# State-space tables as outer products of shared power tables, with masks and signs on ScalarE

## The chip, the cores and the metric

The kernel runs on one core of one Trainium2 chip. The core has five engines that run their own instruction queues side by side: TensorE (PE; its weight loads are PEld), VectorE (DVE), ScalarE (ACT), GpSimd (POOL) and SyncE (SP), which issues the DMAs. The metric is the device time of one execution in microseconds, lower is better. All numbers are fp32.

## The reference, cut to what matters

The model is a trunk of two residual layers over 1024 positions and 1024 features: attention beside a short convolution, a gated feed-forward, a state-space mixer, a second gated feed-forward. Only the parameters of the state-space mixer are touched here:

```
dt = exp(log_step); mag = exp(lr * dt)
ar, ai = mag * cos(li * dt), mag * sin(li * dt)
zr, zi = (nr * lr + ni * li) / den, (ni * lr - nr * li) / den
bbar_r = zr * b_re - zi * b_im ; bbar_i = zr * b_im + zi * b_re
state[s] = a * state[s-1] + bbar @ u[s]        (complex, 64 groups of 16 channels, 64 states each)
y[s] = c_re @ state_r[s] - c_im @ state_i[s] + d_skip * u[s]
```

The kernel runs this scan in chunks of 8 steps. For that it needs tables: `bbar * a^k` and `c * a^k` for k = 0 to 8, and for every group a rotation table with 128 powers of the phase of `a^8`, one for each chunk.

## The kernel before, in words

Activations stay transposed in eight tiles `xT[f]` of 128 features by 1024 positions. Every large product is made in three passes of split operands. A *unit* (`mm_unit`, L175) gives 128 channels by 1024 positions in two PSUM banks `pu` out of 48 matmuls of 128x512. A `down` step (L190) adds two hidden rows into all eight `xT[f]`, 12 matmuls and two PSUM banks `pd` for each f, and VectorE adds the banks to `xT` (L193).

The first feed-forward runs 11 groups of four units and, from the second group on, one `down`: gate, value, gate, value, down. VectorE takes each unit out of PSUM (L759, which frees its two banks), filters it (L757, L762, L764) and multiplies the value with the gate (L808). GpSimd makes low parts of weights (`wl`, L154) and of the gated product (`gl`, L810). PSUM has eight banks, so PE can run ahead of VectorE by eight banks and no more.

Beside this, the state-space tables are computed as a background: the generator `stages()` is advanced by one stage at eight places of each group (`background`): ahead of each of the four units, and after every second f of the down. `base()` prepares the powers of `a`, `z` and the phases `w` in rows of 128x32 (a few stages). Then come 16 *units of the tables*, `unit(q)`, of three stages each, and 16 *turns*, `turns(q)`, of one stage each. A scheduler puts the rows of all of this into one order for each engine, and every engine works off its order strictly in sequence.

In `unit(q)` the tile `z[j]` (j: real, imaginary) holds inputs (w = 0) and outputs (w = 1) for two pairs of groups and nine powers. It is filled by doubling: `cmul` is a complex product of six VectorE rows (L1042 to L1047), and it is called with `a`, `a^2`, `a^4` on 64, 128 and 256 columns, then with `a^8` for the last power. PE turns part of it (`pet`, L1085); VectorE changes a sign (L1092) and forms masked copies `bd` (L1096); PE multiplies both into `pk` (L1102); ScalarE copies `pk`, and stores leave. `turns(q)` fills 128 columns from eight by four more `cmul`.

Of the kernel before, what the change touches and what calls it, by code (L numbers as in the profile page):

```python
# [44 lines left out]
# first columns of the gains and filters  # L45
# [5 lines left out]
def hybrid_trunk_kernel(ctx: ExitStack, tc: tile.TileContext, xt, gains, mix_w_in, w_uq, w_ukv, q_gain, k_gain,  # L51
# [129 lines left out]
    def down(gts, ws, after=None, skip=0):  # L181
        """Adds the products of the rows of ws; the first row is left out for the first skip blocks of features."""
# [14 lines left out]
    class Boundary:  # L197
        """Splits x * gain for the products and gathers the row statistics."""
# [22 lines left out]
        def stats(self):  # L221
            """Row statistics; the function returned broadcasts them to all partitions."""
# [10 lines left out]
    def first_units(ws, xs, bd, rbpool):  # L233
        """Three units beside the row statistics: the first two as the inputs appear."""
# [72 lines left out]
    pps.close()  # L307
    with phase("pc") as pC, tc.tile_pool(name="psa", bufs=1, space=PSUM, reuse_waits="tile") as pa:
# [8 lines left out]
        # compressed projections, natural layout  # L317
# [35 lines left out]
        # up-projection weights of queries, keys and values  # L353
# [14 lines left out]
        def c_products(kind, p):  # L368
            """Compressed queries, or keys and values, of two blocks of rows."""
# [61 lines left out]
        class Step:  # L431
            """Queries, keys and values of two heads and half of the rows."""
# [139 lines left out]
        class Item:  # L572
            """One head and one block of queries."""
# [64 lines left out]
        def row_down(k, f):  # L638
            """One block of features of the output projection's rows k."""
# [107 lines left out]
    def ffn(layer, bd, rbpool, open_pool, gtile, down_last, background=lambda: None, first=None):  # L747
# [30 lines left out]
        def unit():  # L778
            """The next unit's products; the weights of the one after it are made ready before they are used."""
# [65 lines left out]
    class Params:  # L845
# [10 lines left out]
        def held(self):  # L856
            """A value of the preparation alone."""
# [89 lines left out]
        def base(self):  # L947
# [30 lines left out]
            for k in (2, 4, 8):  # L978
                self.a[k] = self.square(self.a[k // 2], (self.t(f"a{k}r"), self.t(f"a{k}i")), False)
            # zero-order hold factor  # L980
# [15 lines left out]
            # chunk decay and chunk rotation  # L996
# [13 lines left out]
            # zero part of the chunk kernel, skip weights  # L1010
# [16 lines left out]
        def cmul(self, dst, src, a, sl, n, eng, rep=1):  # L1027
            """dst = src * a, with a per pair of groups, n columns each."""
# [9 lines left out]
            for j in range(4):  # L1038
                c = self.pool.tile([P, 256], F32, tag=f"cm{j}", name=f"cm{j}")[:, 0:rep * q * n]
# [7 lines left out]
            eng.tensor_tensor(out=dst[1], in0=t[2], in1=t[3], op=ALU.add)  # L1047

# [9 lines left out]
        def unit(self, q):  # L1058
            sl = slice(2 * q, 2 * q + 2)
            bt, ct = self.loaded  # L1060
            # (inputs | outputs), pair, power, channel
            z = [self.pool.tile([P, 2, 2, 9, GC], F32, tag=f"z{j}", name=f"z{j}") for j in range(2)]
            ps = psum("pct")
            nc.tensor.transpose(ps[:, 0:64], ct.rearrange("p j s -> p (j s)"), ident[0:64, 0:64])
            pv = ps[:, 0:64].rearrange("p (t g c) -> p t g c", t=2, g=2)
            for j in range(2):
                for g in range(2):
                    nc.scalar.activation(z[j][64 * g:64 * g + 64, 1, :, 0, :], pv[64 * j:64 * j + 64, :, g, :], AF.Copy)
            self.cmul([z_[:, 0, :, 0, :] for z_ in z], bt, self.z, sl, GC, V)
# [4 lines left out]
            for k in (1, 2, 4):  # L1074
                n = GC * k
                self.cmul([z_[:, :, :, n:2 * n] for z_ in zf], [z_[:, :, :, 0:n] for z_ in zf],
                          self.a[k], sl, n, V, rep=2)
            self.cmul([z_[:, 1, :, 8, :] for z_ in z], [z_[:, 1, :, 0, :] for z_ in z], self.a[8], sl, GC, V)
            yield
            # inputs to chunk states, turned  # L1080
# [10 lines left out]
            # kernel of the chunk  # L1091
            V.tensor_scalar(out=z[1][:, 1], in0=z[1][:, 1], scalar1=-1.0, scalar2=None, op0=ALU.mult)  # L1092
            bd = [self.pool.tile([P, 2, 2, GC], F32, tag=f"bd{j}", name=f"bd{j}") for j in range(2)]
            for j in range(2):
                for g in range(2):
                    V.tensor_scalar(out=bd[j][:, :, g, :], in0=z[j][:, 0, :, 0, :], scalar1=self.hv[:, g:g + 1],  # L1096
                                    scalar2=None, op0=ALU.mult)
# [11 lines left out]
            def store():  # L1109
# [3 lines left out]
                # chunk states to outputs  # L1113
# [10 lines left out]
        def turns(self, q):  # L1124
            """Rotation table of two pairs of groups."""
            sl = slice(2 * q, 2 * q + 2)
            wt = [self.pool.tile([P, 2, NCH], F32, tag=f"wt{j}", bufs=2, name=f"wt{j}") for j in range(2)]
            for j in range(2):
                V.tensor_copy(out=wt[j][:, :, 0:8], in_=self.w8[j][:, sl, :])
            for k in (8, 16, 32, 64):  # L1130
                self.cmul([w_[:, :, k:2 * k] for w_ in wt], [w_[:, :, 0:k] for w_ in wt], self.w[k], sl, k, V)
# [10 lines left out]
        def run(self):  # L1142
            """The stages; what a stage stores leaves at the start of the next one."""
# [6 lines left out]
        def stages(self):  # L1150
            yield from self.base()
            self.loaded = self.load(0)
            yield
# [5 lines left out]
            V.memset(self.w8[0][:, :, 0:1], 1.0)  # L1159
            V.memset(self.w8[1][:, :, 0:1], 0.0)  # L1160
            for k in (1, 2, 4):
                self.cmul([x_[:, :, k:2 * k] for x_ in self.w8], [x_[:, :, 0:k] for x_ in self.w8],
                          self.w[k], slice(0, NP), k, V)
# [46 lines left out]
    ud = dp.tile([KT, P, L, NCH], F32, name="ud")  # L1210
    gd = dp.tile([KT, P, L, NCH], F32, name="gd")
    with ExitStack() as p5s:
# [4 lines left out]
        def enter(m, ps):  # L1217
            """Inputs of 128 channels, to be turned by way of memory."""
# [10 lines left out]
        def turn_inputs(m):  # L1229
            """The inputs of 128 channels with the steps of a chunk on the partitions."""  # L1230
# [23 lines left out]
        def states(m):  # L1254
            """States at the chunks' starts: the chunks' inputs, turned, scanned and turned back."""
# [104 lines left out]
        def gated(j, k0, k1):  # L1360
            """Part of one of the gated unit's first products."""
# [77 lines left out]
def layout(inputs):  # L1439
    """The inputs as the kernel takes them: features on the rows of x, all gains and filters as columns."""  # L1440
# [43 lines left out]
```

## Time and profile before

| what | value |
|---|---|
| time, median of 3 runs (lowest, highest) | 2395.21 us (2392.81, 2395.78) |
| span of the profiled execution | 2393.0 us |
| PE busy | 2308.6 us, 96% |
| VectorE busy | 1585.3 us, 66% |
| ScalarE, GpSimd busy | 776.4 us, 790.9 us |
| mean granted PE clock | 0.984 of full speed |

The span runs from the first instruction to the last of one profiled execution; the time of a run is measured from outside. No time of its own is recorded for the profiled execution; the median of the runs lies 2.2 us above its span. Busy shares are means over stages whose limits differ.

### The profile page before, as it was taken

What the parts mean: (1) busy time and instruction counts of PE and PEld (TensorE: products, weight loads), DVE (VectorE), ACT (ScalarE), POOL (GpSimd) and SP (SyncE); (2) the same over time, 40 slices, a digit from 0 to 9 for tenths busy, and PEclk for the clock granted to TensorE, in tenths of its full rate; (3) what the DMA queues carried; (4) which work ended last, traced back from release to release, by engine and by line L of the source; (5) the groups of instructions that cost most, each with busy time, mean ns of one, the idle gap of its engine ahead of it and who ended that gap; (6) DMA issues with size and microseconds to landing.
All of it is one profiled execution on the core that took longest, in us unless ns stands there. A gap on an engine that the chain in (4) does not pass through costs nothing.

```text
span 2393.0 us, 30439 instructions
## 1 busy us (share of the span) xinstructions
PE 2308.6 (96%) x11492; PEld 1922.9 (80%) x11492; DVE 1585.3 (66%) x3202; ACT 776.4 (32%) x1290; POOL 790.9 (33%) x539
## 2 busy tenths in 40 slices
PE   8999899999999999999999978999999999999999
PEld 6889888888778777787878867788888888888887
DVE  6344677786978878888988487333565665555655
ACT  4112565664223222222223255322322222222221
POOL 3321444444223222222215344333232323322320
PEclk9999999999999999999999998999999999999999
DMA  4111000012112222223332387411111101111111
GB/s 152 44 46 46 1 10 10 10 54 71 37 54 77 66 70 68 51 73 85 93 93 75 103 228 232 116 53 44 53 49 49 51 29 53 53 54 44 53 44 71
DMA packets 215282, 159.57 MB, mean 67 GB/s; under 512 B 24352, under 2 KB 199776, under 8 KB 215136
## 3 DMA queue, kind: packets, MB, share of 16 engines
q1 hardware_dynamic: 215136, 157.63, 22.9%
q8 instruction: 90, 1.47, 0.3%
q14 instruction: 56, 0.46, 0.1%
HBM read 131.44 MB, written 30.34 MB: 68 GB/s over the span
## 4 chain that ended last, share of the span: by engine, by line
PE 56%; DVE 8%; DMA 2%; issue 2%; POOL 1%; ACT 1%; SPq 0%; DVEq 0%; POOLq 0%; ACTq 0%
PE pu L175 38%; PE pd L190 16%; DVE c L764 1%; DMA cs<-csd 1%; DVE c L762 1%; DVE cm L1042 1%; DVE xT L193 1%; DVE cm L1045 1%; DVE cm L1044 1%; DVE c L808 1%; DVE u L759 0%; DMA raw<-in_ffn_w_up_dram 0%; DVE cm L1043 0%; POOL ss L1285 0%; PE pk L1102 0%
## 5 line engine op out<-in xcount | busy, mean ns | idle before, releaser
L154 POOL TENSOR_TENSOR wl<-raw,wh 128x1024 fp32r<-128x1024 f32 (+1 forms) x181 | 448.8, 2481 | 919.5 <-ACT wh L153 376.3
L175 PE MATMUL pu<-f_h,wh 128*128 128x512 f32 x1408 | 437.6, 392 | 0.0
L175 PE MATMUL pu<-f_h,wl 128*128 128x512 f32 x1408 | 435.4, 390 | 0.0
L175 PE MATMUL pu<-f_l,wh 128*128 128x512 f32 x1408 | 434.5, 390 | 0.0
L153 ACT ACTIVATE wh<-raw 128x1024 fp32r<-128x1024 f32 (+1 forms) x183 | 192.1, 1054 | 653.5 <-PE pu L175 406.7
L193 DVE TENSOR_TENSOR xT<-pd,xT 128x512 f32<-128x512 f32 x400 | 254.4, 682 | 106.2 <-PE pd L190 105.8
L759 DVE TENSOR_TENSOR u<-pu,f_rb 128x512 f32<-128x512 f32 x176 | 113.7, 685 | 298.0 <-PE pu L175 294.1
L175 PEld LDWEIGHTS pu<-f_h,wl 128*128 128x128 f32 x1408 | 265.1, 188 | 55.8 <-issue 0.6
L175 PEld LDWEIGHTS pu<-f_l,wh 128*128 128x128 f32 x1408 | 264.9, 188 | 55.5
L175 PEld LDWEIGHTS pu<-f_h,wh 128*128 128x128 f32 x1408 | 263.8, 188 | 56.6 <-issue 2.5
L190 PE MATMUL pd<-gh,wh 128*128 128x512 f32 x704 | 224.2, 399 | 13.0 <-DVE u L759 7.1
L810 POOL TENSOR_TENSOR gl<-c,gh 128x512 fp32r<-128x512 f32 x88 | 115.4, 1333 | 340.1 <-ACT gh L809 340.1
L190 PE MATMUL pd<-gh,wl 128*128 128x512 f32 x704 | 219.6, 393 | 0.0
L190 PE MATMUL pd<-gl,wh 128*128 128x512 f32 x704 | 219.5, 393 | 0.0
L190 PEld LDWEIGHTS pd<-gh,wh 128*128 128x128 f32 x704 | 132.5, 190 | 46.6 <-DVE xT L193 9.1
L762 DVE SCALAR_TENSOR_TENSOR c<-u,vec,c 128x512 f32<-128x512 f32 x176 | 161.3, 950 | 9.3 <-ACT c L761 9.0
L190 PEld LDWEIGHTS pd<-gh,wl 128*128 128x128 f32 x704 | 133.2, 189 | 29.2 <-issue 0.4
L190 PEld LDWEIGHTS pd<-gl,wh 128*128 128x128 f32 x704 | 133.4, 189 | 28.4
L761 ACT ACTIVATE c<-u,vec 128x512 f32<-128x512 f32 x176 | 118.9, 717 | 84.8 <-DVE u L759 77.4
L809 ACT ACTIVATE gh<-c 128x512 fp32r<-128x512 f32 x88 | 53.6, 631 | 248.7 <-DVE c L808 171.8
L764 DVE SCALAR_TENSOR_TENSOR c<-u,vec,c 128x512 f32<-128x512 f32 x176 | 133.7, 794 | 0.2
L757 DVE COPY u<-u 128x2 f32<-128x2 f32 x88 | 123.1, 1399 | 0.0
(442 smaller groups left out, 3715.3 us busy)
## 6 DMA issues: line engine op xcount, KB each, us to landing
raw<-in_ffn_w_up_dram SPq DMA_DIRECT2D x88, 512.0 KB, 3.7
raw<-in_ffn_w_down_dram SPq DMA_DIRECT2D x44, 512.0 KB, 4.5
raw<-in_w_glu_dram SPq DMA_DIRECT2D x16, 512.0 KB, 3.8
raw<-in_mix_w_in_dram SPq DMA_DIRECT2D x14, 512.0 KB, 3.7
xT<-in_xt_dram SPq DMA_DIRECT2D x8, 512.0 KB, 7.7
raw<-in_mix_w_out_dram SPq DMA_DIRECT2D x8, 512.0 KB, 3.5
cpd<-z SPq DMA_DIRECT2D x64, 64.0 KB, 2.1
etd<-et SPq DMA_DIRECT2D x32, 128.0 KB, 1.8
```

Of the source, the lines that this page charges most:

```text
L153: nc.scalar.activation(h[:, 0:n], raw[:, 0:n], AF.Copy)
L154: eng.tensor_tensor(out=l[:, 0:n], in0=raw[:, 0:n], in1=h[:, 0:n].bitcast(F32), op=ALU.subtract)
L175: nc.tensor.matmul(ps[hf], lhsT=w[wi][:, P * k:P * k + P], rhs=xs[k][xi][:, HALVES[hf]], start=(k == 0 and wi == 0 and xi == 0), stop=(k = ...
L190: nc.tensor.matmul(ps[hf], lhsT=ws[i][wi][:, P * f:P * f + P], rhs=gts[i][xi][:, HALVES[hf]], start=(i == first and wi == 0 and xi == 0), ...
L193: nc.vector.tensor_tensor(out=xT[f][:, HALVES[hf]], in0=ps[hf], in1=xT[f][:, HALVES[hf]], op=ALU.add)
L757: nc.vector.tensor_copy(out=u[:, 0:2], in_=u_last[:, HALF:HALF + 2])
L759: nc.vector.tensor_tensor(out=u[:, 2:HALF + 2], in0=ps[hf], in1=rb[:, HALVES[hf]], op=ALU.mult)
L761: nc.scalar.activation(c, u[:, 2:HALF + 2], AF.Copy, scale=cwcol(layer, 2, m))
L762: nc.vector.scalar_tensor_tensor(out=c, in0=u[:, 1:HALF + 1], scalar=cwcol(layer, 1, m), in1=c, op0=ALU.mult, op1=ALU.add)
L764: nc.vector.scalar_tensor_tensor(out=c, in0=u[:, 0:HALF], scalar=cwcol(layer, 0, m), in1=c, op0=ALU.mult, op1=ALU.add)
L809: nc.scalar.activation(gh[:, cols], cv[hf], AF.Copy)
L810: nc.gpsimd.tensor_tensor(out=gl[:, cols], in0=cv[hf], in1=gh[:, cols].bitcast(F32), op=ALU.subtract)
```

## The change

Three edits. (1) In `unit(q)` a source `sr[j]` holds the two starting column blocks, and a new function `outer` forms all powers at once as products of `sr` with a shared table `apow` of `a^0` to `a^8`; six VectorE rows for the inputs (256 columns) and six for the outputs (288 columns) take the place of four `cmul` calls. (2) The sign is folded in (ScalarE copies with scale -1, and `conj` swaps an addition and a subtraction), so L1092 goes, and ScalarE forms `bd` from `sr`. (3) `turns(q)` is one `outer` of two shared tables, `w8` (8 powers) and the new `w16` (16 powers). The tables `apow` and `w16` are made once by `powers`. The temporaries `cm0` to `cm3` grow from 256 to 288 columns. Comments and docstrings are left out of the listing below.

```diff
@@
-            for k in (2, 4, 8):
+            for k in (2, 4):
                 self.a[k] = self.square(self.a[k // 2], (self.t(f"a{k}r"), self.t(f"a{k}i")), False)
...
+        def outer(self, dst, src, tab, shape, conj=False):
...
+            V.tensor_tensor(out=dst[0], in0=src[0], in1=tab[0], op=ALU.mult)
+            V.tensor_tensor(out=t[0], in0=src[1], in1=tab[1], op=ALU.mult)
+            V.tensor_tensor(out=dst[1], in0=src[1], in1=tab[0], op=ALU.mult)
+            V.tensor_tensor(out=t[1], in0=src[0], in1=tab[1], op=ALU.mult)
+            V.tensor_tensor(out=dst[0], in0=dst[0], in1=t[0], op=ALU.add if conj else ALU.subtract)
+            V.tensor_tensor(out=dst[1], in0=dst[1], in1=t[1], op=ALU.subtract if conj else ALU.add)
+
+        def powers(self, tab, steps):
+
+            V.memset(tab[0][:, :, 0:1], 1.0)
+            V.memset(tab[1][:, :, 0:1], 0.0)
+            for first, n, to, a in steps:
+                self.cmul([x_[:, :, to:to + n] for x_ in tab], [x_[:, :, first:first + n] for x_ in tab],
+                          a, slice(0, NP), n, V)
...
         def unit(self, q):
...
+            sr = [self.pool.tile([P, 2, 2, GC], F32, tag=f"sr{j}", name=f"sr{j}") for j in range(2)]
...
-                    nc.scalar.activation(z[j][64 * g:64 * g + 64, 1, :, 0, :], pv[64 * j:64 * j + 64, :, g, :], AF.Copy)
-            self.cmul([z_[:, 0, :, 0, :] for z_ in z], bt, self.z, sl, GC, V)
+                    nc.scalar.activation(sr[j][64 * g:64 * g + 64, 1], pv[64 * j:64 * j + 64, :, g, :], AF.Copy,
+                                         scale=-1.0 if j else 1.0)
+            self.cmul([s_[:, 0] for s_ in sr], bt, self.z, sl, GC, V)
+            bd = [self.pool.tile([P, 2, 2, GC], F32, tag=f"bd{j}", name=f"bd{j}") for j in range(2)]
+            for j in range(2):
+                for g in range(2):
+                    nc.scalar.activation(bd[j][:, :, g, :], sr[j][:, 0], AF.Copy, scale=self.hv[:, g:g + 1])
             yield
...
-            for k in (1, 2, 4):
-                n = GC * k
-                self.cmul([z_[:, :, :, n:2 * n] for z_ in zf], [z_[:, :, :, 0:n] for z_ in zf],
-                          self.a[k], sl, n, V, rep=2)
-            self.cmul([z_[:, 1, :, 8, :] for z_ in z], [z_[:, 1, :, 0, :] for z_ in z], self.a[8], sl, GC, V)
+            for w, n in ((0, 8), (1, 9)):
+                sh = [P, 2, n, GC]
+                self.outer([z_[:, w, :, 0:n, :] for z_ in z],
+                           [s_[:, w].unsqueeze(2).broadcast_to(sh) for s_ in sr],
+                           [a_[:, sl, 0:n].unsqueeze(3).broadcast_to(sh) for a_ in self.apow], sh, conj=w == 1)
             yield
...
-            V.tensor_scalar(out=z[1][:, 1], in0=z[1][:, 1], scalar1=-1.0, scalar2=None, op0=ALU.mult)
...
-                    V.tensor_scalar(out=bd[j][:, :, g, :], in0=z[j][:, 0, :, 0, :], scalar1=self.hv[:, g:g + 1],
-                                    scalar2=None, op0=ALU.mult)
...
         def turns(self, q):
...
-            for j in range(2):
-                V.tensor_copy(out=wt[j][:, :, 0:8], in_=self.w8[j][:, sl, :])
-            for k in (8, 16, 32, 64):
-                self.cmul([w_[:, :, k:2 * k] for w_ in wt], [w_[:, :, 0:k] for w_ in wt], self.w[k], sl, k, V)
+            sh = [P, 2, 16, 8]
+            self.outer([w_.rearrange("p t (m n) -> p t m n", n=8) for w_ in wt],
+                       [w_[:, sl, :].unsqueeze(2).broadcast_to(sh) for w_ in self.w8],
+                       [w_[:, sl, :].unsqueeze(3).broadcast_to(sh) for w_ in self.w16], sh)
...
+            self.powers(self.apow, ((1, 1, 2, self.a[1]), (1, 2, 3, self.a[2]), (1, 4, 5, self.a[4])))
...
+            self.powers(self.w8, [(0, k, k, self.w[k]) for k in (1, 2, 4)])
+            self.powers(self.w16, [(0, k, k, self.w[8 * k]) for k in (1, 2, 4, 8)])
```

The order of instructions moves with it; three places matter below. The first is VectorE's order at the end of a `down`, in the eighth unit of the tables, before (`z0_8875`, `z1_8876` are its two `z` tiles; `xT5` to `xT7` are the last three f of the down, and PE multiplies `pk` right after the last of them):

```order
L1044 TENSOR_TENSOR cm2_8964<-z1_8876,a8r_6692 128x32
L1045 TENSOR_TENSOR cm3_8965<-z0_8875,a8i_6693 128x32
L1046 TENSOR_TENSOR z0_8875<-cm0_8962,cm1_8963 128x2x16
L193 TENSOR_TENSOR xT7_92<-pd_8972,xT7_92 128x512
L1047 TENSOR_TENSOR z1_8876<-cm2_8964,cm3_8965 128x2x16
L193 TENSOR_TENSOR xT7_92<-pd_8973,xT7_92 128x512
L1092 TENSOR_SCALAR z1_8876<-z1_8876 128x288
L1042 TENSOR_TENSOR cm0_9099<-bt0_8925,zr_6703 128x32
```

and after, where the same unit's tiles are `z0_8744` and `z1_8745`:

```order
L1058 TENSOR_TENSOR om1_8818<-sr0_8746,ap1_6926 128x288
L1059 TENSOR_TENSOR z0_8744<-z0_8744,om0_8817 128x288
L193 TENSOR_TENSOR xT5_90<-pd_8770,xT5_90 128x512
L193 TENSOR_TENSOR xT5_90<-pd_8771,xT5_90 128x512
L1060 TENSOR_TENSOR z1_8745<-z1_8745,om1_8818 128x288
L1042 TENSOR_TENSOR cm0_8947<-bt0_8802,zr_6697 128x32
L1047 TENSOR_TENSOR sr1_8940<-cm2_8949,cm3_8950 128x32
L1043 TENSOR_TENSOR cm1_8948<-bt1_8803,zi_6698 128x32
L1046 TENSOR_TENSOR sr0_8939<-cm0_8947,cm1_8948 128x32
L1056 TENSOR_TENSOR om0_9052<-sr1_8940,ap1_6926 128x256
L193 TENSOR_TENSOR xT6_91<-pd_8786,xT6_91 128x512
L193 TENSOR_TENSOR xT6_91<-pd_8787,xT6_91 128x512
```

The last write of `z1` stood behind the first half of `xT7` and was followed by the sign (L1092) behind the second half; now it stands behind `xT5`, and no sign follows. Counted on PE's order, `pk` then stands 24 large matmuls behind the `pd` that this `xT5` waits for, where before it stood 5 behind that of `xT7`.

The second is VectorE's order in the turns, ahead of the last unit of a group (L759 frees its banks), before; 45 rows of turns stand there between L755 and L759, of which these are the last 11:

```order
L1043 TENSOR_TENSOR cm1_12417<-wt1_12393,w32i_6833 128x64
L1044 TENSOR_TENSOR cm2_12418<-wt1_12393,w32r_6832 128x64
L1045 TENSOR_TENSOR cm3_12419<-wt0_12392,w32i_6833 128x64
L1046 TENSOR_TENSOR wt0_12392<-cm0_12416,cm1_12417 128x2x32
L1047 TENSOR_TENSOR wt1_12393<-cm2_12418,cm3_12419 128x2x32
L1042 TENSOR_TENSOR cm0_12426<-wt0_12392,w64r_6844 128x128
L1043 TENSOR_TENSOR cm1_12427<-wt1_12393,w64i_6845 128x128
L1044 TENSOR_TENSOR cm2_12428<-wt1_12393,w64r_6844 128x128
L1045 TENSOR_TENSOR cm3_12429<-wt0_12392,w64i_6845 128x128
L1046 TENSOR_TENSOR wt0_12392<-cm0_12426,cm1_12427 128x2x64
L1047 TENSOR_TENSOR wt1_12393<-cm2_12428,cm3_12429 128x2x64
L759 TENSOR_TENSOR u_12349<-pu_12293,f0_rb_6041 128x512
```

and after, where all rows of turns between L755 and L759 are shown:

```order
L755 MEMSET u_11715 128x2
L1057 TENSOR_TENSOR wt1_11759<-w81_10839,w160_10840 128x256
L1055 TENSOR_TENSOR wt0_11804<-w80_10838,w160_10840 128x256
L1060 TENSOR_TENSOR wt1_11759<-wt1_11759,om1_11761 128x256
L1056 TENSOR_TENSOR om0_11806<-w81_10839,w161_10841 128x256
L1057 TENSOR_TENSOR wt1_11805<-w81_10839,w160_10840 128x256
L1058 TENSOR_TENSOR om1_11807<-w80_10838,w161_10841 128x256
L1059 TENSOR_TENSOR wt0_11804<-wt0_11804,om0_11806 128x256
L1060 TENSOR_TENSOR wt1_11805<-wt1_11805,om1_11807 128x256
L1056 TENSOR_TENSOR om0_11853<-w81_10839,w161_10841 128x256
L1058 TENSOR_TENSOR om1_11854<-w80_10838,w161_10841 128x256
L759 TENSOR_TENSOR u_11715<-pu_11659,f0_rb_6041 128x512
```

Ahead of this L759 there are 10 rows of turns now.

The third is VectorE's order in `base()`, ahead of the L759 of the last unit of the second group, before; `w4` and `w8` are phases, and 51 rows of tables stand there:

```order
L881 SCALAR_TENSOR_TENSOR w8i_6809<-w4r_6796,w4i_6797 128x32
L868 TENSOR_TENSOR w8r_6808<-scr_6298 128x32
L868 TENSOR_TENSOR scr_6298<-w8i_6809 128x32
L868 TENSOR_TENSOR scr_6298<-w8r_6808 128x32
L868 TENSOR_TENSOR scr_6298<-scr_6298 128x32
L876 TENSOR_SCALAR scr_6298<-scr_6298 128x32
L759 TENSOR_TENSOR u_6579<-pu_6523,f0_rb_6041 128x512
```

and after, where 55 rows stand there:

```order
L868 TENSOR_TENSOR w2i_6779<-w2i_6779,scr_6298 128x32
L1055 TENSOR_TENSOR z0_7033<-sr0_7035,ap0_6925 128x2x128
L868 TENSOR_TENSOR scr_6298<-w2r_6778,w2i_6779 128x32 x2
L881 SCALAR_TENSOR_TENSOR w4i_6791<-w2r_6778,w2i_6779 128x32
L1056 TENSOR_TENSOR om0_7148<-sr1_7036,ap1_6926 128x256
L868 TENSOR_TENSOR w4r_6790<-scr_6298 128x32
L868 TENSOR_TENSOR scr_6298<-w4i_6791 128x32
L1058 TENSOR_TENSOR om1_7149<-sr0_7035,ap1_6926 128x256
L759 TENSOR_TENSOR u_6579<-pu_6523,f0_rb_6041 128x512
```

The squares of the phases that stood here have moved behind L759, and the powers of `a` and the first rows of `outer` have come in front of it.

## Rows read from the trace of the kernel before

**Rows 1.** Page of the profile, parts 1 (busy us, share) and 2 (tenths in 40 slices).

```profile
PE 2308.6 (96%) x11492; PEld 1922.9 (80%) x11492; DVE 1585.3 (66%) x3202; ACT 776.4 (32%) x1290; POOL 790.9 (33%) x539
...
DVE  6344677786978878888988487333565665555655
```

**Rows 2.** View of waits, PE, 560 to 1380 us: total, times, longest.

```profile
PE pk L1102 <- DVE z L1092: 7.4, 2, 3.7
PE pd L190 <- DVE u L759: 7.1, 2, 5.9
PE pd L190 <- DVE xT L193: 5.4, 3, 4.1
```

**Rows 3.** View of stretches, PE: length, busy (rows), granted clock, DMA share, GB/s.

```profile
636.50:642.80 6.30, 6.30 (x14) 0.51 0.00 1
871.10:875.10 4.00, 3.99 (x14) 0.57 0.51 129
1207.30:1217.00 9.70, 4.32 (x17) 0.95 0.47 102
1217.00:1222.80 5.80, 5.71 (x13) 0.50 0.00 0
```

**Rows 4.** Timeline of PE, 636 to 1218 us: start, length, row, [idle before <- releaser].

```profile
636.47 1.39 PE L190 MATMUL pd<-gh,wh 128*128 128x512 f32 x2 [5.86 <-DVE u L759]
...
871.11 0.85 PE L1102 MATMUL pk<-z,bd 128*32 128x128 f32 x6 [3.64 <-DVE z L1092]
...
1217.09 1.39 PE L190 MATMUL pd<-gh,wh 128*128 128x512 f32 x2 [4.10 <-DVE xT L193]
```

**Rows 5.** Timeline of DVE, 626 to 643 us, and of POOL in the same stretch (last row).

```profile
626.08 0.18 DVE L868 TENSOR_TENSOR scr<-hold 128x32 f32<-128x32 f32 x1
...
627.96 2.39 DVE L868 TENSOR_TENSOR w1r<-scr 128x32 f32<-128x32 f32 x1
...
635.72 1.28 DVE L759 TENSOR_TENSOR u<-pu,f_rb 128x512 f32<-128x512 f32 x2
...
641.12 2.48 DVE L193 TENSOR_TENSOR xT<-pd,xT 128x512 f32<-128x512 f32 x4
...
627.89 2.40 POOL L154 TENSOR_TENSOR wl<-raw,wh 128x1024 fp32r<-128x1024 f32 x1 [4.62 <-ACT wh L153]
```

**Rows 6.** Timeline of DVE, 836 to 871 us: one unit of the tables, then the sign.

```profile
836.47 0.21 DVE L1044 TENSOR_TENSOR cm<-z,a1r 128x64 f32<-128x64 f32 x1
...
837.01 0.28 DVE L1042 TENSOR_TENSOR cm<-z,a2r 128x128 f32<-128x128 f32 x1
...
838.23 0.41 DVE L1042 TENSOR_TENSOR cm<-z,a4r 128x256 f32<-128x256 f32 x1
...
840.24 0.18 DVE L1042 TENSOR_TENSOR cm<-z,a8r 128x32 f32<-128x32 f32 x1
...
840.87 0.18 DVE L1042 TENSOR_TENSOR cm<-bt,zr 128x32 f32<-128x32 f32 x1
...
870.76 0.29 DVE L1092 TENSOR_SCALAR z<-z 128x288 f32<-128x288 f32 x1
```

**Rows 7.** Timeline of DVE, 1093 to 1210 us: the first power table, then one turn.

```profile
1093.40 0.22 DVE L1042 TENSOR_TENSOR cm<-w,w1r 128x32 f32<-128x32 f32 x1 [2.31 <-DMA cpd<-z]
...
1096.19 0.32 DVE L1129 COPY wt<-w 128x16 f32<-128x16 f32 x3
...
1205.62 0.17 DVE L1042 TENSOR_TENSOR cm<-wt,w8r 128x16 f32<-128x16 f32 x1
...
1208.86 1.28 DVE L759 TENSOR_TENSOR u<-pu,f_rb 128x512 f32<-128x512 f32 x2
```

**Rows 8.** View of stretches, two groups: length, then PE PEld DVE ACT POOL busy, clock, DMA.

```profile
917.40:988.00 70.60, 70.31 (x317) 55.86 (x316) 60.58 (x152) 18.96 (x39) 20.66 (x10) 1.00 0.23 61
1134.00:1199.90 65.90, 65.84 (x290) 54.01 (x289) 61.29 (x193) 15.97 (x23) 17.89 (x10) 1.00 0.34 89
```

**Rows 9.** View by lines, ACT, 640 to 1090 us: count | busy, mean ns | idle before.

```profile
L1068 ACT ACTIVATE z<-pct 64x32 f32<-64x32 f32 x64 | 12.1, 189 | 29.6 <-PE pct L1064 25.4 <-DMA bt<-in_b_im_dram 3.4
```

More of the change, by code (lines that the diff above doesn't have):

```diff
@@ L1038, in cmul @@
             for j in range(4):
-                c = self.pool.tile([P, 256], F32, tag=f"cm{j}", name=f"cm{j}")[:, 0:rep * q * n]
+                c = self.pool.tile([P, 288], F32, tag=f"cm{j}", name=f"cm{j}")[:, 0:rep * q * n]
                 t.append(c.rearrange("p (q n) -> p q n", q=q) if rep == 1 else
@@ L1047, in cmul @@
             eng.tensor_tensor(out=dst[1], in0=t[2], in1=t[3], op=ALU.add)
+        def outer(self, dst, src, tab, shape, conj=False):
+            n = int(np.prod(shape[1:]))
+            names = ("q m n", {"q": shape[1], "m": shape[2]})
+            t = [self.pool.tile([P, 288], F32, tag=f"cm{j}", name=f"om{j}")[:, 0:n].rearrange(
+                "p (q m n) -> p q m n", **names[1]) for j in range(2)]
+            V.tensor_tensor(out=dst[0], in0=src[0], in1=tab[0], op=ALU.mult)
[10 more added lines that the diff above has]
+                          a, slice(0, NP), n, V)
         def load(self, q):
@@ L1090, in unit @@
                 ets.append(et)
-            V.tensor_scalar(out=z[1][:, 1], in0=z[1][:, 1], scalar1=-1.0, scalar2=None, op0=ALU.mult)
-            bd = [self.pool.tile([P, 2, 2, GC], F32, tag=f"bd{j}", name=f"bd{j}") for j in range(2)]
-            for j in range(2):
-                for g in range(2):
-                    V.tensor_scalar(out=bd[j][:, :, g, :], in0=z[j][:, 0, :, 0, :], scalar1=self.hv[:, g:g + 1],
-                                    scalar2=None, op0=ALU.mult)
             pk = psum("pk")
@@ L1127, in turns @@
             wt = [self.pool.tile([P, 2, NCH], F32, tag=f"wt{j}", bufs=2, name=f"wt{j}") for j in range(2)]
-            for j in range(2):
-                V.tensor_copy(out=wt[j][:, :, 0:8], in_=self.w8[j][:, sl, :])
-            for k in (8, 16, 32, 64):
-                self.cmul([w_[:, :, k:2 * k] for w_ in wt], [w_[:, :, 0:k] for w_ in wt], self.w[k], sl, k, V)
+            sh = [P, 2, 16, 8]
+            self.outer([w_.rearrange("p t (m n) -> p t m n", n=8) for w_ in wt],
+                       [w_[:, sl, :].unsqueeze(2).broadcast_to(sh) for w_ in self.w8],
+                       [w_[:, sl, :].unsqueeze(3).broadcast_to(sh) for w_ in self.w16], sh)
             def store():
@@ L1152, in stages @@
             self.loaded = self.load(0)
+            self.apow = [self.pool.tile([P, NP, 9], F32, tag=f"ap{j}", name=f"ap{j}") for j in range(2)]
+            for j in range(2):
+                V.tensor_copy(out=self.apow[j][:, :, 1], in_=self.a[1][j])
+            self.powers(self.apow, ((1, 1, 2, self.a[1]), (1, 2, 3, self.a[2]), (1, 4, 5, self.a[4])))
             yield
@@ L1158, in stages @@
             self.w8 = [self.pool.tile([P, NP, 8], F32, tag=f"w8{j}", name=f"w8{j}") for j in range(2)]
[L1159 to L1163, printed above, removed]
+            self.w16 = [self.pool.tile([P, NP, 16], F32, tag=f"w16{j}", name=f"w16{j}") for j in range(2)]
+            self.powers(self.w8, [(0, k, k, self.w[k]) for k in (1, 2, 4)])
+            self.powers(self.w16, [(0, k, k, self.w[8 * k]) for k in (1, 2, 4, 8)])
             yield
```

## The prediction

> **What bounds the kernel now.** I read the page first. PE is busy 96% of the span [rows 1], so the kernel can only gain where PE stands still or runs at a lower clock; what VectorE saves elsewhere costs nothing now and gives nothing back. VectorE's slices show where that may be: they stand at 7 to 9 tenths from the eleventh slice to the 22nd [rows 1], which is the first feed-forward with the tables in its background. The next view is therefore PE's waits in that stretch. Three kinds matter [rows 2]: `pk` waits twice for the sign of `z` (L1092), 7.4 us in all; `pd` waits for L759, which frees a unit's banks, 7.1 us; and `pd` waits for L193, which frees those of the down, 5.4 us. The timeline gives their places [rows 4]: 5.86 us before 636.47 in the preparation (`base`), 3.64 us before 871.11 and the same again before 1089, and 4.10 us before 1217.09 in the turns, where a wait of 1.2 us for L759 (the 7.1 us less 5.86) comes first.
>
> A wait costs more than itself. Behind each the granted clock is at half, 1.2 GHz instead of 2.4, for some microseconds: 0.51 of full speed over 6.30 us behind the first, 0.57 over 4.0 us behind the `pk` wait, 0.50 over 5.8 us behind the last, where PE is busy throughout [rows 3]. What is lost is the missing share of each stretch: 6.3 x 0.49 = 3.1, 4.0 x 0.43 = 1.7 for each `pk`, 5.8 x 0.50 = 2.9 us, and 9.7 x 0.05 = 0.5 around the short wait.
>
> So the whole sum within reach of this change is: `base` 5.9 + 3.1 = 9.0 us; the two `pk` 7.4 + 3.4 = 10.8 us; the turns 1.2 + 4.1 + 0.5 + 2.9 = 8.7 us. The rest of the span has other causes.
>
> **Why VectorE is late there.** A group of the feed-forward lasts 70.6 us with units of the tables beside it, of which GpSimd works 20.7 us, and 65.9 us with turns, GpSimd 17.9 us; in both PE does not stand still [rows 8]. While GpSimd works on a tile of 128x1024, a VectorE row on two tiles stands still: the row at 627.96 took 2.39 us beside a GpSimd row of 2.40 us that began at 627.89, where its neighbours take 0.2 us [rows 5]. The feed-forward itself takes 5.40 us of VectorE for a value unit (635.72 to 641.12), 1.2 us less for a gate, and 0.60 us for each of 16 L193 [rows 5]: 2 x 5.4 + 2 x 4.2 + 9.6 = 28.8 us. What is left for the tables is 70.6 - 20.7 - 28.8 = 21.1 us in a group with units and 65.9 - 17.9 - 28.8 = 19.2 us in one with turns, and eight stages have to go into each.
>
> The Trainium skill, page "SBUF — State Buffer", section "Who interferes with whom", says that a VectorE instruction with two inputs in SBUF and a GpSimd instruction that reads SBUF exclude each other, and the later one waits until the first is done. By that rule, the trace agrees (2.39 beside 2.40 us). Without it the room for turns would be 37.1 us, every stage would fit, and the wait in the turns would need another cause that this change might not touch: the gain would be the `pk` terms alone.
>
> **What the change removes and adds.** A row of n columns costs, start to start and without GpSimd, what the unit at 836 us shows [rows 6]: 0.135 us for 64 columns (four rows in 0.54), 0.20 for 128 (six in 1.22), 0.335 for 256 (six in 2.01), 0.105 for 32 (six in 0.63). With 32 pairs and a stride, three sizes of 32, 64 and 128 take 2.79 us together [rows 7].
> - Unit of the tables, before: input product 0.6, doubling 0.8 + 1.2 + 2.0 + 0.6, sign 0.2, four masks at no less than 0.1 each: 5.9 us. After: 0.6, six rows of 256 (2.0) and six of 288 columns (0.377 each by proportion, 2.3): 4.9 us. Eight stages are 2.7 units: 15.7 us before and 13.1 after, both within 21.1.
> - Turn, before: 1205.62 to 1208.86, 3.24 us, and two copies, 3.4 in all [rows 7]. After: six rows of 256 columns, 2.0 us. Eight turns are 27.3 us before, 8 over the room of 19.2, and 16.1 after, 3 under it. Two groups of turns follow each other.
> - Shared tables, once: `apow` adds 2.8 us in `base`, `w16` 2.8 + 2.0 = 4.8 us ahead of the first turns; one square (`a^8`) goes, 0.4 us.
>
> No row here has two operands spread out at once, as `outer` has. From below its cost is the 0.335 us of a row with one such operand, from above twice that. I take the lower, since the columns are the same and these rows already read one operand with a zero step.
>
> **The `pk` waits (gain 10.8 us).** By the order of the eighth unit, `pk` stands 24 large matmuls behind the L193 after which `z1` is finished, and before 5. At 288 large matmuls in a group of 65.9 us [rows 8], 0.23 us each, that is 5.5 us of lead in place of 1.1. The other units that had a lead of 10 or 12 did not wait; the least lead of the 16 units is now 24. What is late next would be `bd`, now on ScalarE: 64 rows like those at 0.189 us [rows 9], 12 us on an engine busy 32% [rows 1], placed a stage ahead of `pk`. Cover: three f of the down at 2.7 us; without it, a `pk` wait as before, 5.4 us.
>
> **The turns (gain 8.7 us).** Ahead of the L759 before the last down stand 10 rows of turns, 3.4 us, where 45 stood. In the first group of turns the tables bring 16.1 + 2.8 + 4.8 = 23.7 us, 4.5 over the room; before it were 27.3 + 2.8, 11 over, and PE had no wait there but `pk`, since eight banks let it run ahead. That `pk` wait also gave VectorE 5.4 us, which it no longer gets: 9.9 over in all, against 11 tolerated. This is close, and I put up to 2 us of new waits there, in the range.
>
> **The wait in `base` (loss 1.5 us).** It stays, since its 51 rows are preparation. Before, they took 9.64 us (626.08 to 635.72), 2.2 of it GpSimd [rows 5], so 0.146 each. After, 33 of them remain (4.8 us), and in come 13 rows of `apow` (0.1 + 0.8 + 1.2), six of the input product (0.6) and three of `outer` (1.0): 8.6 us against 7.4, and one more `outer` row (0.3) behind L759. PE's wait ends when L759, and then the first L193, are through: 1.5 us later. ScalarE's `bd` now stands ahead of the weight copy that releases the GpSimd row, so this row falls behind L759 and not ahead of it, 2.2 us taken from one wait and given to the next. Bounds: -2.2 us, if it delays nothing there, to 1.5 + 3.4 us, if another 6.8 us pass at half clock.
>
> **Sum.** 10.8 + 8.7 - 1.5 = 18.0 us. The profiled span is 2393.0 us, the median 2395.2 us. So the span should be 2375.0 us and the median 2377.2 us; I say 2377. VectorE's busy time should fall by some 16 + 22 - 7 = 31 us and by what its rows no longer spend blocked, at 540 rows fewer.
>
> **Rivals.**
> - The first group of turns, or the end of `base`, brings a new wait of the size of the old one in the turns. For it: 10 us over the room there. Against it: the second group falls from 8 over to 3 under. 8.7 us given back: 2386.
> - The time in `base` is not small change: the longer stretch, and ScalarE's queue with `bd` ahead of weight copies, bring new waits in each of the first units until nothing is left. For it: ScalarE works strictly in order and already waited 25.4 us for PE before such rows [rows 9]. Against it: rows ahead of `pk` stand several f earlier. Three or four waits of 5 us: 2390 to 2400, no difference.
> - Slower: `outer` rows cost twice, 0.67 and 0.75 us each. Then a unit costs 0.6 + 4.0 + 4.5 = 9.1 us, eight stages 24.4, 3.3 us over the room in each of six groups, 20 us, and a turn 4.0 us, 5 us more a group than before, 10 us; less the 11 us that the banks bore before: 2414. It decides at (21.1 / 2.7 - 0.6) / 12 = 0.60 us a row. Against it: [rows 6].
> - Everything gains: `base` loses its wait too, through the moved GpSimd row: 2368.
>
> **Numbers.** Forecast (2372 to 2383) 0.60; a new wait, 2386, 0.20; nothing gained 0.11; slower 0.06; also `base` 0.03. A measurement of this kernel can tell about 0.2%, 4.8 us, from no change. Faster 0.83, same 0.11, slower 0.06. The range, 2368 to 2390, takes in the bounds of `base`, the new wait and little more.
>
> **What would show it.** PE's waits have no `pk` row of microseconds, and no `pd` wait near the second group of turns; the half-clock stretches at 871, 1089 and 1217 are gone, and the one near 636 stays. `outer` rows of 256 columns read 0.41 us, 0.335 start to start. VectorE's slices 12 to 21 fall by a tenth or more. I am wrong if `outer` rows stand 0.60 us apart, if `pk` waits for ScalarE's `bd`, or if PE waits in the stretch of the first turns.

## The result, and the profile after

| | before | after |
|---|---|---|
| time, median of 4 runs (lowest, highest) | 2394.01 us (2391.43, 2395.78) | 2366.84 us (2364.72, 2371.39) |
| ratio, 95% interval | | 0.9887 (0.9873 to 0.9901) |
| span of the profiled execution | 2393.0 us | 2365.8 us |
| mean granted PE clock | 0.984 | 0.988 |

The change makes the kernel 27.2 us faster, where 18.0 were forecast; the time lies 1.2 us below the range. The page of the changed kernel, its parts 1 and 2 (against [rows 1]):

```profile
PE 2293.3 (97%) x11492; PEld 1914.1 (81%) x11492; DVE 1531.4 (65%) x2654; ACT 790.9 (33%) x1354; POOL 795.5 (34%) x539
...
DVE  6344677786978777878767486323656566555655
```

VectorE lost 548 rows and 53.9 us of busy time. PE's waits from 560 to 1350 us (line, releaser: total, times, longest; against [rows 2]):

```profile
PE pd L190 <- DVE xT L193: 3.7, 2, 3.5
PE pd L190 <- DVE u L759: 2.9, 1, 2.9
PE f_pb L126 <- DVE f_dg L119: 0.8, 1, 0.8
```

No `pk` row is left and none in the turns; the two long waits stand in the preparation, as before. Stretches of PE, as in [rows 8] and [rows 3]: the same two groups, then the last wait of the preparation and what follows it (length, busy, granted clock, DMA share, GB/s):

```profile
912.30:981.60 69.30, 69.30 (x317) 1.00 0.25 69
1120.50:1186.10 65.60, 65.60 (x289) 1.00 0.40 104
639.20:642.70 3.50, 0.00 (x0) 0.79 0.00 0
642.70:648.10 5.40, 5.39 (x12) 0.50 0.00 0
```

The first row is the one to look at. In [rows 8] this group lasted 70.60 us with PE busy for 70.31 of them, and I took that as its floor. It now lasts 69.3 with as many large matmuls. The preparation has kept its half clock of 1.2 GHz: 5.4 us at 0.50 behind the wait.

Next, VectorE: the end of a unit of the tables, then the end of the turns ahead of an L759 (start, length, row), which answer to [rows 6] and [rows 7].

```profile
858.81 0.45 DVE L1056 TENSOR_TENSOR om<-sr,ap 128x288 f32<-128x288 f32 x1
859.17 0.45 DVE L1057 TENSOR_TENSOR z<-sr,ap 128x288 f32<-128x288 f32 x1
...
1185.50 0.41 DVE L1056 TENSOR_TENSOR om<-w,w 128x256 f32<-128x256 f32 x1
1185.84 0.41 DVE L1058 TENSOR_TENSOR om<-w,w 128x256 f32<-128x256 f32 x1
1186.17 1.27 DVE L759 TENSOR_TENSOR u<-pu,f_rb 128x512 f32<-128x512 f32 x2
```

A row with both operands spread out takes 0.41 us for 256 columns and starts 0.33 to 0.34 us behind the one before: the lower of the two prices in the prediction.

**Where the 27.2 us are.** PE's large matmuls stand in the same sequence in both kernels, so each stage can be measured from its first matmul to that of the next (a group from the first L190 of one `down` to that of the next; the first stage from the span's start, the last to the end of PE's last matmul). The differences are taken before rounding:

| stage, us | before | after | difference | forecast |
|---|---|---|---|---|
| attention and short convolution | 530.0 | 532.3 | +2.3 | 0 |
| preparation, to the second `down` | 169.0 | 169.6 | +0.7 | +1.5 |
| 3rd and 6th group with units (the `pk` waits) | 75.9, 74.3 | 70.7, 68.4 | -11.1 | -10.8 |
| 1st, 2nd, 4th, 5th group with units | 70.5, 72.1, 70.5, 71.7 | 69.3, 70.5, 69.3, 70.5 | -5.4 | 0 |
| two groups with turns, then to the end of the first feed-forward | 65.9, 74.6, 44.5 | 65.6, 65.6, 44.0 | -9.9 | -8.7 |
| state-space stage | 188.6 | 184.4 | -4.2 | 0 |
| the rest | 880.7 | 880.7 | 0.0 | 0 |

(PE's last matmul is not the end of the span, hence 27.6 here.) Within the first feed-forward it is 25.6 us. The two open questions are the 5.4 us of groups that had no wait of a microsecond, and whether the +2.3 and -4.2 us outside belong to the change.

**The 5.4 us.** The stream of large matmuls is broken where PE turns a unit of the tables (`pet`) and multiplies it (`pk`). Timeline of PE in the first group, before:

```profile
713.61 0.88 PE L1085 MATMUL pet<-ident,z 128*128 128x128 f32 x4 [0.29 <-DVE z L1046]
714.42 0.41 PE L1102 MATMUL pk<-z,bd 128*32 128x128 f32 x2
714.75 0.73 PE L190 MATMUL pd<-gh,wh 128*128 128x512 f32 x2
...
717.24 0.63 PE L1102 MATMUL pk<-z,bd 128*32 128x128 f32 x6
```

and after:

```profile
716.10 0.60 PE L1112 MATMUL pet<-ident,z 128*128 128x128 f32 x4
716.63 0.64 PE L1123 MATMUL pk<-z,bd 128*32 128x128 f32 x8
```

Before, `pet` waited 0.29 us and `pk` came in two pieces, two products while `z1` was late and six after ten large matmuls; after, it is one piece. Counting for every break the time from the last large start ahead to the first one behind, less the 0.23 us of a large matmul, one whole piece costs 1.10 us, and the two pieces here 1.60 + 0.65. In the six groups there were 34 breaks of 34.1 us in all before, and there are 30 of 21.2 us after. Four units were in two pieces, one each in the first, third, fourth and sixth group; two of these carried the long `pk` waits. In the second and fifth group the loss is in waits of 0.3 to 0.8 us, the longest of them in the `down`, before:

```profile
780.12 1.10 PE L190 MATMUL pd<-gh,wh 128*128 128x512 f32 x2 [0.79 <-DVE xT L193]
...
998.31 1.10 PE L190 MATMUL pd<-gh,wh 128*128 128x512 f32 x2 [0.51 <-DVE xT L193]
```

34.1 - 21.2 = 12.9 us, and the 3.4 us of half clock behind the two `pk` waits make 16.3 of the 16.4 us that the six groups lost (435.0 to 418.6).

### The profile page after: what moved, and what is told of

The parts are those of the page before. It is cut to its first block, busy times and chain, and to the rows that moved or that the text cites. A ratio compares the mean times of both kernels' runs of the same rounds, so it can differ in the third digit from the quotient of the medians.

```text
span 2365.8 us, 29954 instructions
## 1 busy us (share of the span) xinstructions
PE 2293.3 (97%) x11492; PEld 1914.1 (81%) x11492; DVE 1531.4 (65%) x2654; ACT 790.9 (33%) x1354; POOL 795.5 (34%) x539
## 4 chain that ended last, share of the span: by engine, by line
PE 85%; DVE 6%; DMA 3%; ACT 2%; issue 2%; POOL 1%; SPq 0%; DVEq 0%; POOLq 0%; ACTq 0%
PE pu L175 53%; PE pd L190 23%; PE pss L586 1%; PE po L634 1%; PE pckv L378 1%; PE pq L446 1%; PE ptp L615 1%; PE pcq L378 1%; PE pda L644 1%; PE pkv L464 1%; DVE nm L595 1%; DMA co<-cpd 1%; DVE a_sq L219 0%; DVE xT L646 0%; DMA ut<-ud 0%
## 5 line engine op out<-in xcount | busy, mean ns | idle before, releaser
L193 DVE TENSOR_TENSOR xT<-pd,xT 128x512 f32<-128x512 f32 x400 | 254.5, 682 | 113.8 <-PE pd L190 113.1
L759 DVE TENSOR_TENSOR u<-pu,f_rb 128x512 f32<-128x512 f32 x176 | 113.6, 686 | 307.4 <-PE pu L175 303.4
L190 PE MATMUL pd<-gh,wh 128*128 128x512 f32 x704 | 221.4, 395 | 6.8 <-DVE xT L193 3.7
L190 PE MATMUL pd<-gl,wh 128*128 128x512 f32 x704 | 218.7, 392 | 0.0
L190 PE MATMUL pd<-gh,wl 128*128 128x512 f32 x704 | 218.3, 391 | 0.0
L190 PEld LDWEIGHTS pd<-gh,wh 128*128 128x128 f32 x704 | 131.5, 189 | 37.7 <-DVE xT L193 5.3
L190 PEld LDWEIGHTS pd<-gh,wl 128*128 128x128 f32 x704 | 132.7, 189 | 28.8
L190 PEld LDWEIGHTS pd<-gl,wh 128*128 128x128 f32 x704 | 132.7, 189 | 28.3
```

The lines of the kernel that those rows point to most:

```text
L190: nc.tensor.matmul(ps[hf], lhsT=ws[i][wi][:, P * f:P * f + P], rhs=gts[i][xi][:, HALVES[hf]], start=(i == first and wi == 0 and xi == 0), ...
L193: nc.vector.tensor_tensor(out=xT[f][:, HALVES[hf]], in0=ps[hf], in1=xT[f][:, HALVES[hf]], op=ALU.add)
L759: nc.vector.tensor_tensor(out=u[:, 2:HALF + 2], in0=ps[hf], in1=rb[:, HALVES[hf]], op=ALU.mult)
```

## The experiments

**The changed kernel again, and the change in two parts.**

> The changed kernel once more, so that the parts below are compared with it on one chip, and to see how much of the 4.2 us that the state-space stage was shorter, and of the 2.2 us that the attention was longer, comes again. Theory (only the first feed-forward changed; the other two differences are chance of DMA arrival and of the clock): 25.4 us less than before, 2368 to 2369, and stage lengths outside the first feed-forward that differ between two profiles of the same code by microseconds. Rival (earlier tables shorten the state-space stage): 27 us or more less, 2366, and that stage again some 4 us shorter than before.

Measured: 2367.06 us, 0.9890 (0.9875 to 0.9905), and the stages of after to within 0.2 us.

```diff
 # units_only, against after
-            self.outer([w_.rearrange("p t (m n) -> p t m n", n=8) for w_ in wt], ...)
...
+            for k in (8, 16, 32, 64):
+                self.cmul([w_[:, :, k:2 * k] for w_ in wt], [w_[:, :, 0:k] for w_ in wt], self.w[k], sl, k, V)
...
-            self.powers(self.w16, [(0, k, k, self.w[8 * k]) for k in (1, 2, 4, 8)])
```

> The change without its turns: the turns are formed by the four products of before, everything else as after. Theory: gain is 11.5 us of the two pk waits with their half clock and 5.0 us of waits under a microsecond and split products in the groups with units, less 0.7 us in the preparation: 15.8 us less than before, 2378; the wait of 4.1 us in the second group of turns comes back. Rival (the small waits belong to something else, and the turns' tables feed the state-space stage): 11 us less, 2383.

```diff
 # turns_only, against before
-            for k in (8, 16, 32, 64):
-                self.cmul([w_[:, :, k:2 * k] for w_ in wt], ...)
+            self.outer([w_.rearrange("p t (m n) -> p t m n", n=8) for w_ in wt], ...)
...
+            self.powers(self.w16, [(0, k, k, self.w[8 * k]) for k in (1, 2, 4, 8)])
```

> The kernel before with only its turns formed as outer products, units by doubling as before. Theory: 9.2 us of the turns' waits and half clock and 0.5 us of small ones: 9.7 us less than before, 2384; both pk waits of 3.7 us stay. Rival (the state-space stage gains from turns that are stored earlier): 14 us less, 2380, with that stage 4 us shorter in the trace. Rival 2 (VectorE in the turns is not what PE waits for): no difference, 2394.

| | us | ratio to before (95%) | preparation | groups with units | turns, to the end |
|---|---|---|---|---|---|
| units only | 2373.99 | 0.9918 (0.9905 to 0.9932) | 169.6 | 69.3 70.5 70.7 69.3 70.5 68.4 | 67.6 68.8 44.0 |
| turns only | 2384.63 | 0.9961 (0.9948 to 0.9973) | 168.9 | 70.5 73.3 75.9 70.5 71.7 74.3 | 65.6 65.6 44.0 |

PE's waits with the turns alone, 560 to 1350 us:

```profile
PE pk L1123 <- DVE z L1113: 7.4, 2, 3.7
PE pd L190 <- DVE u L759: 5.9, 1, 5.9
PE pd L190 <- DVE xT L193: 3.0, 3, 2.1
```

The units alone give 19.2 us, 3.4 more than expected; the small waits do belong to the units. The turns alone give 8.6 us, both `pk` waits stay at 7.4. (In that run the second group with units is 1.2 us longer than before, by a wait for `xT` of 2.1 us where one of 0.79 us stood; why an edit to the turns does this stays open.) The miss in the units is instructive: with the *old* turns behind the *new* units, the second group of turns takes 68.8 us, not 74.6. PE waits 1.4 us in the first group of turns, where it had not waited, and 2.6 us in the second, where 1.2 + 4.1 us stood; the granted clock stays at 1.00 behind both:

```profile
1132.13 1.10 PE L190 MATMUL pd<-gh,wh 128*128 128x512 f32 x2 [1.39 <-DVE xT L193]
...
1200.91 1.10 PE L190 MATMUL pd<-gh,wh 128*128 128x512 f32 x2 [2.58 <-DVE xT L193]
```

The turns' rows are the same, but the scheduler placed them anew: 38 of them stand between the last two units ahead of the second of these waits, where 49 stood. That this is what shortens the wait is read from the order; no run changes the order alone. Half of the turns' term (4.7 of 9.9 us) is gone with the first edit, so the two terms do not add.

**Which of the edits in the units.**

```diff
 # outer_only, against after: sign and masks on VectorE, ahead of pk
+            V.tensor_scalar(out=z[1][:, 1], in0=z[1][:, 1], scalar1=-1.0, ...)
...
+                    V.tensor_scalar(out=bd[j][:, :, g, :], in0=sr[j][:, 0], scalar1=self.hv[:, g:g + 1], ...)
 # masks_only, against before: doubling stays
-            V.tensor_scalar(out=z[1][:, 1], in0=z[1][:, 1], scalar1=-1.0, ...)
+            nc.scalar.activation(z[1][:, 1], z[1][:, 1], AF.Copy, scale=-1.0)
```

(In the second, the masks also go to ScalarE, as in the change.)

> The changed kernel with its second edit undone: sign and masks are VectorE rows again, at their old place ahead of pk; outer products in units and turns as after. Theory (what counts is how long before pk the last row of z1 stands): the sign stands 12 large matmuls ahead of pk in the worst unit, where it was 5 before and is 24 after, and units with 10 or 12 did not wait before, so pk does not wait; some 12 us more of VectorE rows spread over six groups are hidden: 2367 to 2369, as after. Rival (masks and sign on ScalarE are what took the waits away): both pk waits with their half clock come back, 11.5 us: 2378.

> The kernel before with the second edit alone: sign and masks on ScalarE, tables by doubling. Theory: the last row of the doubling still stands behind the first half of xT7, 5 large matmuls ahead of pk, and the sign follows it on ScalarE; each pk wait shrinks by about half a microsecond and stays above 3 us; 1 to 3 us less than before, 2390 to 2392. Rival (the second edit brings the gain of the units): pk waits gone, 2375. The state-space stage is looked at too: if it follows the turns of before, its length is 188 to 190 us here and 184 to 186 us in the kernels of this call with the new turns.

Outer only: 2366.78 us, 0.9883 (0.9870 to 0.9897), every group with units as after. Masks only: 2392.59 us, 0.9990 (0.9981 to 0.9999). Its waits:

```profile
PE pd L190 <- DVE u L759: 7.3, 2, 6.0
PE pk L1101 <- ACT z L1096: 7.3, 2, 3.7
PE pd L190 <- DVE xT L193: 4.7, 2, 4.1
```

`pk` waits as long as before, now for ScalarE, since the doubling ahead of it is as late as it was; the half microsecond that I had expected is hardly there. So the outer products bring the whole gain, and moving sign and masks adds nothing to it. By itself the second edit is not idle, though: what it gives, 2.3 us and hardly more than the noise, stands in the second and fifth group, which take 70.4 us each in both profiles of this kernel (72.1 and 71.7 before). The small waits there go with either edit; the `pk` waits and the products in two pieces go with the outer products alone. In the preparation the second edit costs: it took 169.6 us after and 168.3 with the masks on VectorE. The rows that say why, from the timeline of all engines of the changed kernel:

```profile
633.33 0.96 ACT L1096 ACTIVATE bd<-sr,hv 128x32 f32<-128x32 f32 x4 [4.65 <-DVE sr L1046]
634.19 1.04 ACT L153 ACTIVATE wh<-raw 128x1024 fp32r<-128x1024 f32 x1
...
635.01 1.31 DVE L759 TENSOR_TENSOR u<-pu,f_rb 128x512 f32<-128x512 f32 x2
635.36 2.39 POOL L154 TENSOR_TENSOR wl<-raw,wh 128x1024 fp32r<-128x1024 f32 x1 [10.22 <-issue]
...
636.21 1.57 DVE L757 COPY u<-u 128x2 f32<-128x2 f32 x1
```

The four masks hold up the weight copy, so GpSimd's row falls behind L759, as the prediction said, and stops the copy of two columns that follows. With the masks on VectorE, the same row of GpSimd ran ahead of L759 and stopped a row of the tables there, and the copy was short:

```profile
627.38 2.40 DVE L876 TENSOR_SCALAR scr<-scr 128x32 f32<-128x32 f32 x1
...
635.04 0.15 DVE L757 COPY u<-u 128x2 f32<-128x2 f32 x1
```

The waits were 5.2 us for L759 and 0.4 us for L193 there, in place of 2.9 and 3.5. That is 0.8 us of the difference; the rest stays open. The Trainium skill, page "SBUF — State Buffer", section "Who interferes with whom", names a second case beside the two inputs of the prediction: a VectorE row in a two-port mode. By that rule a copy, which has one input, can be held up too; the trace agrees (1.57 us, to the end of GpSimd's row at 637.75), though no row tells the mode.

**The price of lateness.**

```diff
 # outer_twice, against after
-            for w, n in ((0, 8), (1, 9)):
+            for w, n in ((0, 8), (0, 8), (1, 9), (1, 9)):
```

> The changed kernel with every outer product of a unit done twice (the second time with the same result), 12 rows and 4.2 us of VectorE more in each unit. It is the price of the rival in which a row costs twice. Theory by the room of a group: eight stages bring 24.3 us into 21.1 us, 3.2 us over in each of six groups, 19 us and some half clock: 2386 or more. Rival (the room is not what sets the waits; where the last rows of z1 stand does, and that lead is still 12 large matmuls in the worst unit): below 2372.

Measured: 2388.97 us, 0.9971 (0.9960 to 0.9981), 22 us more than after. PE's waits:

```profile
PE pk L1123 <- DVE z L1059: 10.4, 6, 4.1
PE pd L190 <- DVE xT L193: 3.8, 5, 1.3
PE pd L190 <- DVE u L759: 2.9, 1, 2.9
```

The groups with units sum to 438.8 us, 20.3 more than after, where the room gave 19. Nothing was spread evenly, though: 70.0, 72.8, 78.0, then 69.9, 72.9, 75.2. Lateness is carried from group to group and is paid mostly in the third of each three. `pk` waits 4.1 us here with a lead of 12 large matmuls by the order, and 0.3 to 0.9 us with a lead of 24; with the masks on VectorE, units with a lead of 12 had no wait. So a lead is worth something only while VectorE keeps up with the order, and the room decides first.

**The wait in the preparation.**

```diff
 # free_base, against after: powers not ahead of the last L759, phases one square for each unit
-                V.tensor_copy(out=self.apow[j][:, :, 1], in_=self.a[1][j])
+                V.scalar_tensor_tensor(out=self.apow[j][:, :, 1], in0=xT[1][:, 0:NP], scalar=0.0,
+                                       in1=self.a[1][j], op0=ALU.mult, op1=ALU.add)
...
                 yield from self.unit(q)
+                if 2 <= q < 11:
+                    k = 2.0 ** (q - 4)
+                    self.w[k] = self.square(self.w[k / 2], ..., True)
 # free_spread, against free_base: inside the same if, ahead of the square
+                    for a in self.w[k / 2]:
+                        V.scalar_tensor_tensor(out=a, in0=xT[1 + 2 * (q % 3)][:, 0:NP], scalar=0.0, in1=a,
+                                               op0=ALU.mult, op1=ALU.add)
```

(Both runs also give the first phase and the squares tiles of their own and shorten the scratch from 12 rows to 8; free_base ties the first phase to `xT1` as well.)

> The changed kernel with the last wait in the preparation taken out: the powers of a take a zero multiple of xT1 as an operand, so that they cannot be placed ahead of the last unit of the first group, and the nine squares of the phases are made one for each unit of the tables, from the second unit on. The results are the same. Theory: the 36 rows of powers, first outer products and phases no longer stand ahead of L759, so the waits of 2.9 and 3.5 us and the half clock behind them, 3.4 us, go: 9.8 us less than after, 2357. Some 90 rows of 0.105 us, 9.5 us in all, go into five groups with 8 us to spare in each, and bring nothing back. Rival: they bring waits back there, 2362 to 2367.

Measured: 2365.28 us, 0.9882 (0.9868 to 0.9895). The preparation fell from 169.6 to 160.8 us, but the second group rose from 70.5 to 76.5:

```profile
775.26 1.39 PE L190 MATMUL pd<-gh,wh 128*128 128x512 f32 x2 [3.26 <-DVE xT L193]
```

Written one to a unit, the squares were all ready early, and the scheduler had put even the last two ahead of a unit at the end of the first group: in the trace 17 of their rows run from 741.38 to an L759 at 748.30. Some need the one just before them and start 0.2 us behind it, and GpSimd stops two of them for 2.4 and 2.3 us:

```profile
741.38 2.38 DVE L869 TENSOR_TENSOR v9r<-scr 128x32 f32<-128x32 f32 x1
...
744.02 2.27 DVE L869 TENSOR_TENSOR scr<-scr 128x32 f32<-128x32 f32 x1
```

The next `down` pays, as the next run confirms. The rival was right, 2365 within its 2362 to 2367.

> The kernel with the free base (2365.3), in whose trace the preparation was 8.9 us shorter but one group of units 6.0 us longer, since the squares of the phases had all run early in that group; now each square takes a zero multiple of another xT of the down before it, and cannot come earlier. Results unchanged. Theory: the group is back at 70.5 us and the preparation stays short: 6 us less, 2359. Rival (any 9 us more in these groups bring a wait): 2363 to 2367.

Measured: 2359.42 us, 0.9850 (0.9837 to 0.9864), the fastest of all; preparation 160.9 us, the groups 69.3, 70.5, 70.7, 69.3, 70.5, 68.4, so the second is back where it was. Its first feed-forward has no half clock left. Waits:

```profile
PE f_pb L126 <- DVE f_dg L119: 0.8, 1, 0.8
PE pd L190 <- DVE xT L193: 0.7, 2, 0.5
PE pu L175 <- POOL wl L154: 0.4, 1, 0.4
```

**The stages outside.**

> The kernel before once more, for the part of the difference that lies outside the first feed-forward. So far the attention took 528.6 to 532.3 us over ten profiles of kernels that are alike there, and the state-space stage 184.3 to 189.8 us; with the turns of before 185.3, 188.6 and 189.8, with the new ones 184.3 to 187.6. Theory (chance): both lie in these ranges again, and the groups of the first feed-forward repeat to 0.1 or 0.2 us: 70.5, 72.1, 75.9, 70.5, 71.7, 74.3, 65.9, 74.6. Rival (the turns of before lengthen the state-space stage): 188 us or more.

Measured: 2394.94 us, ratio 1.0001 (0.9989 to 1.0013); attention 529.8, state-space stage 188.7 us; the groups repeat to 0.2 us but for the sixth, 75.0.

> Second profile of the kernel with the second edit alone, for its state-space stage (first profile 185.3 us), which has the turns of before. Theory (chance): anywhere from 184 to 190 us. Rival (the stage follows the turns): 188 us or more, and the 185.3 was an exception.

> Second profile of the kernel with the turns alone (first profile 186.0 us in the state-space stage). Theory (chance): anywhere from 184 to 190 us. Rival (the stage follows the turns): 184 to 187 us.

> Second profile of the change without its turns (first profile 189.8 us in the state-space stage). Theory (chance): anywhere from 184 to 190 us. Rival (the stage follows the turns): 188 us or more.

Measured, one run each: 2392.77, 2386.00 and 2371.57 us; the state-space stage took 187.6, 185.4 and 185.9 us. All profiles together:

| state-space stage, us | |
|---|---|
| turns of before | 188.6, 188.7 (before), 185.3, 187.6 (masks only), 189.8, 185.9 (units only) |
| turns of after | 184.4, 184.4 (after), 186.0, 185.4 (turns only), 186.8, 187.6, 186.2, 186.5 (the others) |

The means, 187.7 and 185.9, differ by 1.8 us, while one and the same kernel differs by 3.9 us between two profiles. The attention, which no kernel here changes, takes 528.6 to 532.3 us. The strong form of the rival (188 us or more with the old turns) has fallen; whether a part of these 1.8 us belongs to the change stays open.

## Why the prediction was right, and where it was wrong

- **The two `pk` waits** (10.8 us): 11.1 measured, and by the mechanism named, an earlier last row of `z`. That it is the outer product and not ScalarE that does it, the two experiments on the edits show.
- **The turns** (8.7 us): 9.9 measured, 9.1 of it in the second group. The 10 rows ahead of L759 are over before PE needs the banks, and the first group of turns brought no new wait, so that rival is out. The experiments add that the first edit alone would have given 4.7 of it.
- **`base`** (+1.5 us): +0.7. The waits are 2.9 and 3.5 us where one of 5.9 was, in the two places foretold. The size was off: the 55 rows ahead of L759 took 7.1 us (627.95 to 635.01), where I had charged 8.6, and the half clock behind is shorter, 5.4 us where 6.3 stood [rows 3].
- **The step that failed** is "in both PE does not stand still" [rows 8]. From it, the four groups without a `pk` wait were given no gain; they gave 5.4 us. A busy share of 70.31 in 70.60 is no floor. In the group of that row, the fourth, the busy time held a small product in two pieces, 2.26 us where one piece costs 1.10; in the second and fifth group there were waits of 0.3 to 0.8 us. Both stand in the trace of before: of the 5.4 us of waits for L193 in [rows 2], the sum took up 4.1 and dropped 0.79 and 0.51. The sentence that units with a lead of 10 or 12 "did not wait" misses the same: those with 10 are the ones in two pieces, with 0.29 us of wait ahead of `pet`, and those with 12 lost 0.4 us in `pk`.
- With 0.8, 0.3, 5.4 and 1.2 us these four make the 7.6 us between 18.0 and 25.6 (unrounded). The remaining 1 to 2 us of the measured 26 to 27 lie within what the stages outside vary by; so do the 1.2 us by which the time lies below the range.
- **What would show it**: the half clock at 871, 1089 and 1217 is gone and stays in the preparation, and rows cost 0.41 and 0.33 to 0.34 us. VectorE's slices 12 to 21 fell by 7 tenths together, not by one each: PE got faster too, and VectorE's share hardly moves. Its busy time fell by 53.9 us, where at least 31 was said.
- **Slower, with rows of twice the price**: the 20 us for the units were about right (20.3 with every outer product done twice). But even so the kernel was 5.9 us faster than before: the rival added its 20 us to the time of before, which already held the 16.4 us that these groups lost with the change. Turns at twice the price, 10 us of that rival, were not tried.

## What to carry to other kernels

When an engine that feeds a saturated TensorE is relieved, do not price only the waits that have a row of microseconds: look at how the stream of large matmuls is broken, count the breaks and their cost, and see in the new order which of them close up. Terms read from one static order do not add when the order is planned anew, and background work that is merely written later is still placed as early as its operands are ready; an operand that comes late holds it where it costs nothing. After a gain, look where the next wait of the same kind stands: here freeing the preparation gave some 7.5 us more.

## What the runs showed of the hardware that was not expected

- An elementwise VectorE row in which one operand repeats a block and the other repeats each element costs no more than one with a single repeated operand: 0.41 us for 128x256, as in [rows 6], starting 0.33 to 0.34 us apart. One of 128x288 takes 0.45 us, 0.36 to 0.37 us apart.
- The same four transposes and eight products cost a stream of 128x512 matmuls 1.10 us in one piece, and 1.60 + 0.65 us in two, of which 0.29 us is a wait.
- Stages that no edit touches vary between profiles by 3.7 us (attention) and 5.5 us (state-space stage, in which the page before shows DMA at 8 and 7 tenths of two slices), while a group of the first feed-forward repeats to 0.1 us where VectorE is on time.
